# Six plain up-projection pairs instead of seven in the conv FFN of a two-layer encoder, the last three of them on the normalised stream

## The chip, the cores and the metric

The kernel runs on one core of one Trainium2 chip. The metric is device microseconds of one execution. TensorE (PE) does the matmuls, VectorE (DVE), ScalarE (ACT) and GpSimd (POOL) the rest, and SyncE (SP) issues the transfers. PEld is PE's loading of weights, which overlaps its matmuls.

## The reference, cut to what matters

Two layers; each has a mixer of two kinds of attention, a cross attention over 256 memory tokens, and a gated FFN with a convolution over positions. The change is in the FFN alone:

```python
def conv_ffn(h, w_up, conv_w, conv_b, w_down):
    u = h @ w_up
    up = jnp.pad(u, ((0, 0), (1, 1), (0, 0)))
    u = up[:, :-2] * conv_w[0] + up[:, 1:-1] * conv_w[1] + up[:, 2:] * conv_w[2] + conv_b
    gate, val = jnp.split(u, 2, axis=-1)
    return (jax.nn.silu(gate) * val) @ w_down
...
x = x + conv_ffn(rms_norm(x, norm_ffn[l]), w_up[l], conv_w[l], conv_b[l], w_down[l])
```

x is 512 positions by 1024 channels in float32; w_up is 1024 x 5632 and w_down 2816 x 1024.

## The kernel before

The stream x is kept transposed: eight tiles xT of 128 channels by 512 positions. Float32 accuracy comes from splitting each operand into hi (x rounded to the PE format fp32r) and lo = x - hi; each product is three matmuls, hi x hi, hi x lo and lo x hi (`mm3`, `product`). ACT writes hi, and DVE or POOL subtracts for lo.

Every call on an engine is first recorded, all at one source line (L404 in the profile). Then a planner sets one order of the whole program, from costs of its own, due times and the free buffers, and each engine runs its part of that order. So the code states what depends on what, and the planner decides where an instruction stands in its engine's queue. What limits it: three raw weight tiles (512 KB each, N_RAW), four hi and four lo weight tiles, 23 tiles called r, 14 tiles called t, two called xg, and eight PSUM banks (four mm, two sc, two tr).

The FFN of a layer computes 22 pairs: pair j is 128 gate channels and the 128 value channels that go with them. There are two ways to compute a pair.

- **Plain pairs** (j below N_PLAIN = 7, in `up_first`). Two gemms, one for each side: 8 channel tiles k, three matmuls each, with 512 columns. They read `ffn.ops`, hi/lo of the stream before its scaling by 1/rms, in the two xg tiles. So they can start before the norm is known; once it is known (`ffn.spread` makes rep in SBUF and a copy in PSUM), DVE multiplies both results by rep (`finish`).
- **Seven-product pairs** (`up`). A Strassen-like scheme on halves of the channels and of the positions: seven products of 4 x 3 matmuls with 256 columns. Its operands `right` come from the normalised stream (built in `operands`: a and b are channel tiles c and c + 4, scaled; hi/lo of parts of a and b, and of four sums t1 to t4). The weight side is built from two raw tiles in `combined`: three parts split into hi/lo in r tiles, and four sums, added by POOL and split in the hi and lo weight tiles by ACT and DVE.

After a pair, `up_finish` does the convolution on ACT and DVE, which reads the PSUM banks and so frees them, then silu(gate) x value; `store` writes hi/lo for the down projection. The stores of the plain pairs come after all plain pairs in the program, most of them into the two xg tiles (the ring), which are free once the last plain pair has read `ffn.ops`; j = 2 and 3 go into r tiles. Grouped down projections (`down_grouped`, 24 matmuls of 512 columns for each row r) are mixed in behind the seven-product pairs by `behind(n)`: row 0 after pair 7, one or two rows after each later pair.

SP issues the weight tiles in the order of the planner. A raw tile's slot is free when all splits and sums that read it are done.

Of the kernel before, what the change touches and what calls it, by code (L numbers as in the profile page):

```python
# [26 lines left out]
KC = D // P  # L27
# [3 lines left out]
D_FF = 2816  # L31
NF = D_FF // P
N_GROUPED = 16
N_PLAIN = 7
N_COLS = 256
BEHIND = 5
EPS = 1e-6
# [21 lines left out]
N_RAW, N_W, AHEAD, AHEAD_HELD, N_WARM, N_LATE, N_FIRST = 3, 4, 2, 5, 7, 4, (12, 22)  # L59


SLOTS = {j: j % KC if j < 8 or j > 11 else (2, 3, 0, 1)[j - 8] for j in range(N_GROUPED)}


def behind(n):

    at = lambda r: (7, 8, 9, 9, 10, 11, 12, 12)[r] if r < 8 else r + BEHIND
    return [r for r in range(N_GROUPED) if at(r) == n]


# [428 lines left out]
def encoder_kernel(ctx: ExitStack, tc: tile.TileContext, t: dict, out: list):  # L499
# [21 lines left out]
    def rtile(shape, dt=F32R):  # L521
        return rpool.tile([P, *shape], dt, tag="r", name=nm("r"), padded_shape=[P, *pad(shape)])
# [7 lines left out]
    def rpair():  # L530

        hl = rtile((2, S))
        return hl[:, 0, :], hl[:, 1, :]
# [13 lines left out]
    f = lambda ap: ap.bitcast(F32)  # L547
# [84 lines left out]
    at = 0  # L632
# [22 lines left out]
    def gemm_T(ps, w, ops, ks, first, last, c=slice(0, P)):  # L655
        wh, wl = w
        for k in ks:
            mm3(ps, wh[:, k, c], wl[:, k, c], *ops[k], k == first, k == last)
# [252 lines left out]
    for l in range(DEPTH):  # L911
# [602 lines left out]
        def up_project(j, side, ks, us):  # L1514
            if us[side] is None:
                us[side] = get_w(("up", j, side)), ps_mm() if j % 4 < 2 else ps_t() if side else ps_s()
            w, pm = us[side]
            gemm_T(pm, w, ffn.ops, ks, 0, KC - 1)

        def up_first():  # L1520


            us = [[None] * 2 for _ in range(N_PLAIN)]
            up_project(0, 0, range(KC - 1), us[0])
            ffn.stat()
            ffn.spread()
            up_project(0, 1, range(KC - 1), us[0])
            for side in range(2):
                up_project(0, side, [KC - 1], us[0])
            up_project(1, 0, range(KC), us[1])  # L1530
            built = operands()
            next(built)
            up_project(1, 1, range(KC), us[1])

            def finish(j):
                pms = [pm for _, pm in us[j]]
                for pm in pms:
                    DVE.tensor_mul(pm, pm, ffn.rep)
                return up_finish(j, pms)

            stores = []
            for j in range(2, N_PLAIN):
                for side in range(2):
                    up_project(j, side, range(KC), us[j])
                next(built, None)
                stores.append(finish(j - 2))
            for j in range(N_PLAIN - 2, N_PLAIN):
                stores.append(finish(j))
            for store in stores:
                store()  # L1550

        H = S // 2
        right = {n: [None] * 4 for n in ("11", "21", "22", "t1", "t2", "t3", "t4")}

        def operands():


            base = []
            for c in range(4):
                xs = []  # L1560
                for k in (c, c + 4):
                    v = tmp()
                    DVE.scalar_tensor_tensor(v, xT[k], par[:, l, G_FFN + k : G_FFN + k + 1], ffn.psum,
                                             op0=ALU.mult, op1=ALU.mult)
                    xs.append(v)
                a, b = xs
                i = c % 2
                if i == 0:
                    base = [rtile((4, H)) for _ in range(3)]
                pair = lambda t: t[:, 2 * i : 2 * i + 2].rearrange("p n q -> p (n q)")  # L1570
                ACT.copy(pair(base[0]), b)
                POOL.tensor_sub(pair(base[1]), b, f(pair(base[0])))
                ACT.copy(base[2][:, i], a[:, :H])
                DVE.tensor_sub(base[2][:, 2 + i], a[:, :H], f(base[2][:, i]))
                right["21"][c], right["22"][c] = ((base[0][:, 2 * i + n], base[1][:, 2 * i + n]) for n in range(2))
                right["11"][c] = base[2][:, i], base[2][:, 2 + i]
                one, two = tmp((2, H)), tmp((2, H))
                POOL.tensor_sub(one[:, 0], a[:, :H], a[:, H:])
                DVE.scalar_tensor_tensor(one[:, 1], one[:, 0], -1.0, b[:, H:], op0=ALU.mult, op1=ALU.subtract)
                POOL.tensor_sub(two[:, 0], b[:, H:], a[:, H:])  # L1580
                DVE.scalar_tensor_tensor(two[:, 1], one[:, 1], -1.0, b[:, :H], op0=ALU.mult, op1=ALU.subtract)
                hi, lo = rtile((4, H)), rtile((4, H))
                for n, v in ((0, one), (2, two)):
                    ACT.copy(hi[:, n : n + 2], v)
                    DVE.tensor_sub(lo[:, n : n + 2], v, f(hi[:, n : n + 2]))
                for n, name in enumerate(("t1", "t2", "t3", "t4")):
                    right[name][c] = hi[:, n], lo[:, n]
                yield
# [47 lines left out]
        def up_finish(j, us, turned=False):  # L1636
            cs = []
            for side in range(2):
                ch = side * NF + j
                u = us[side]  # L1640
                w = [par[:, l, CW + i * 2 * NF + ch : CW + i * 2 * NF + ch + 1] for i in range(3)]
                if turned and side:
                    w = [minus[:, l, i * NF + j : i * NF + j + 1] for i in range(3)]
                cc = tmp()
                ACT.activation(cc, u, AF.Identity, bias=par[:, l, CB + ch : CB + ch + 1], scale=w[1])
                for wi, dst, src in (
                    (w[0], slice(8, S), slice(0, S - 8)),
                    (w[0], slice(1, 8), slice(S - 8, S - 1)),
                    (w[2], slice(0, S - 8), slice(8, S)),
                    (w[2], slice(S - 8, S - 1), slice(1, 8)),  # L1650
                ):
                    DVE.scalar_tensor_tensor(cc[:, dst], u[:, src], wi, cc[:, dst], op0=ALU.mult, op1=ALU.add)
                cs.append(cc)
            ACT.activation(cs[0], cs[0], AF.Silu)
            DVE.tensor_mul(cs[0], cs[0], cs[1])

            def store():
                if j < N_GROUPED and j not in (2, 3):
                    if not ring:
                        ring.extend(xpool.tile([P, KC, S], F32R, tag="xg", name=nm("xg"), bufs=2) for _ in range(2))  # L1660
                    acts[j] = [v[:, SLOTS[j]] for v in ring]
                else:
                    acts[j] = rpair()
                hi, lo = acts[j]
                ACT.copy(hi, cs[0])
                DVE.tensor_sub(lo, cs[0], f(hi))

            return store
# [298 lines left out]
```

## Time and profile before

| what | us |
|---|---|
| median of 3 runs | 1303.92 |
| lowest and highest | 1303.55, 1304.28 |
| the profiled execution's own time | 1303.15 |
| its span, first to last instruction | 1301.1 |
| layer 0: the first gemm of the second plain pair starts | 312.37 |
| layer 0: the first seven-product pair starts | 377.90 |
| layer 1: the first seven-product pair starts | 1020.30 |

Times inside the execution are us from the start of the span. Groups are named out<-in by the program's tiles: sc<-xg is a matmul that writes an sc bank and reads an xg tile, t<-mm,par a part of the convolution, mm<-mm,rep the scaling of a plain pair's result. A row of the timeline gives the start, the length, engine, line, operation, tiles, shape and count; in brackets stand the engine's idle time before it and what ended it. Starts of matmuls that follow each other give the true time of one: their lengths overlap.

### The profile page before, as it was taken

The page shows a single profiled execution, that of the slowest core. Times are in us where ns is not written, and L with a number is a line of the kernel's source. Part 1 is how long each engine was busy: PE and PEld are TensorE (multiplying, and loading weights), DVE is VectorE, ACT ScalarE, POOL GpSimd, SP SyncE. Part 2 cuts the span into 40 slices and gives each one's busy share as a digit, 9 for nine tenths or more (in the row PEclk, how much of TensorE's full clock was granted, in tenths as well). Part 3 has the DMA queues.
Part 4 walks back from the last instruction along what each step waited for, and adds up shares of the span by engine and source line. Part 5 has one row for each costly group of instructions (what it writes and reads, how often), then busy time and mean ns, then how long its engine had stood idle before and what let it go on. Part 6 is the DMA issues. An engine that isn't in the chain of part 4 may idle for free.

```text
span 1301.1 us, 20672 instructions
## 1 busy us (share of the span) xinstructions
PE 1291.9 (99%) x7485; PEld 1135.6 (87%) x7485; DVE 1066.1 (82%) x1999; ACT 777.3 (60%) x1510; POOL 655.8 (50%) x523
## 2 busy tenths in 40 slices
PE   9999999999999999999999999999999999999998
PEld 8898888888889999999888988888888999999997
DVE  8679886768999998878655887866789998997784
ACT  7776686555565555555537867865655645554552
POOL 4565866716743334334626566765367224542260
PEclk9999999999999999999999999999999999999999
DMA  8651313313323333233356322232133233333231
GB/s 286 194 171 49 114 49 97 96 35 113 98 81 98 110 134 98 66 97 113 122 162 179 114 81 82 66 99 96 49 98 97 82 113 115 112 99 98 77 118 65
DMA packets 42901, 137.47 MB, mean 106 GB/s; under 512 B 5040, under 2 KB 8496, under 8 KB 42800
## 3 DMA queue, kind: packets, MB, share of 16 engines
q1 hardware_dynamic: 42224, 135.51, 33.3%
q8 instruction: 59, 0.97, 0.3%
q10 hardware_dynamic: 576, 0.66, 0.1%
q14 instruction: 42, 0.34, 0.1%
HBM read 126.18 MB, written 2.10 MB: 99 GB/s over the span
## 4 chain that ended last, share of the span: by engine, by line
PE 94%; POOL 1%; DVE 1%; issue 1%; ACT 1%; DMA 0%; SPq 0%; DVEq 0%; POOLq 0%
PE mm L404 55%; PE sc L404 20%; PE tr L404 20%; POOL lo L404 1%; ACT t L404 0%; POOL s L404 0%; DVE t L404 0%; DVE r L404 0%; DVE s L404 0%; DMA xT<-in_w 0%; ACT r L404 0%; POOL t L404 0%; DVE mm L404 0%; DVE sc L404 0%; POOL r L404 0%
## 5 line engine op out<-in xcount | busy, mean ns | idle before, releaser
L404 POOL TENSOR_TENSOR lo<-raw,hi 128x512 fp32r<-128x512 f32 (+2 forms) x168 | 265.8, 1599 | 185.8 <-ACT hi L404 179.9
L404 PE MATMUL mm<-xg,hi 128*128 128x512 f32 (+1 forms) x1026 | 319.3, 391 | 0.0
L404 POOL TENSOR_TENSOR t<-raw,raw 128x512 f32<-128x512 f32 x60 | 86.5, 1463 | 290.4 <-DMA raw<-in_w 213.8
L404 ACT CAST hi<-raw 128x512 fp32r<-128x512 f32 (+2 forms) x216 | 163.8, 784 | 111.8 <-PE mm L404 35.2
L404 PEld LDWEIGHTS mm<-xg,hi 128*128 128x128 f32 x1026 | 188.4, 188 | 35.5
L404 PE MATMUL mm<-xg,lo 128*128 128x512 f32 (+1 forms) x513 | 199.7, 389 | 0.0
L404 PE MATMUL mm<-r,hi 128*128 128x512 f32 (+1 forms) x608 | 192.0, 388 | 0.0
L404 PE MATMUL sc<-r,r 128*128 128x256 f32 (+1 forms) x736 | 131.8, 310 | 0.9 <-ACT t L404 0.9
L404 PEld LDWEIGHTS mm<-r,hi 128*128 128x128 f32 x608 | 111.9, 188 | 21.6 <-DVE xg L404 0.8
L404 PE MATMUL mm<-r,lo 128*128 128x512 f32 (+1 forms) x336 | 123.3, 367 | 0.0
L404 PEld LDWEIGHTS mm<-xg,lo 128*128 128x128 f32 x513 | 96.3, 188 | 20.2
L404 PEld LDWEIGHTS sc<-r,r 128*128 128x128 f32 x736 | 103.5, 191 | 7.4 <-ACT t L404 2.0
L404 PE MATMUL mm<-hi,xg 128*128 128x512 f32 (+1 forms) x384 | 108.1, 358 | 0.0
L404 PE MATMUL sc<-r,hi 128*128 128x256 f32 (+1 forms) x752 | 106.7, 288 | 0.0
L404 POOL TENSOR_SCALAR t<-t,s 128x512 f32<-128x512 f32 (+1 forms) x112 | 67.0, 613 | 71.8 <-DVE s L404 71.7
L404 POOL TENSOR_TENSOR t<-t,raw 128x512 f32<-128x512 f32 x60 | 99.5, 1658 | 4.7
L404 PEld LDWEIGHTS sc<-r,hi 128*128 128x128 f32 x752 | 97.0, 192 | 1.4
L404 PE MATMUL tr<-r,lo 128*128 128x256 f32 x720 | 96.2, 283 | 0.0
L404 PE MATMUL tr<-r,r 128*128 128x256 f32 x720 | 96.1, 283 | 0.0
L404 PEld LDWEIGHTS tr<-r,r 128*128 128x128 f32 x720 | 92.6, 191 | 2.3
L404 PEld LDWEIGHTS tr<-r,lo 128*128 128x128 f32 x720 | 90.7, 192 | 0.0
L404 ACT ACTIVATE t<-sc,s,s 128x512 f32<-128x512 f32 (+1 forms) x96 | 68.1, 711 | 29.2 <-DVE s L404 25.8
(158 smaller groups left out, 2756.3 us busy)
## 6 DMA issues: line engine op xcount, KB each, us to landing
raw<-in_w SPq DMA_DIRECT2D x207, 512.0 KB, 3.6
r<-r SPq DMA_DIRECT2D x30, 256.0 KB, 3.6
r<-in_bias SPq DMA_DIRECT2D x16, 384.0 KB, 4.6
raw<-in_w SPq DMA_DIRECT2D x8, 384.0 KB, 3.8
r<-in_memT SPq DMA_DIRECT2D x4, 512.0 KB, 7.2
xT<-in_w SPq DMA_DIRECT2D x7, 256.5 KB, 4.6
r<-in_w SPq DMA_DIRECT2D x9, 128.0 KB, 4.1
t<-in_memT SPq DMA_DIRECT2D x4, 256.0 KB, 6.1
```

What stands on the lines that cost most here:

```text
L404: call(*args, **kwargs)
```

## The change

Pair j = 6 becomes a seven-product pair. `operands` first builds the eight normalised tiles in full width, hi and lo (`normed`, eight r tiles), and the operands 11, 21 and 22 of the seven products become views of them; the sums t1 to t4 come afterwards, one c for each of the pairs j = 2 to 5. Plain pairs j = 3 to 5 read `normed` and need no multiplication by rep; j = 0 to 2 stay as they were. So the xg tiles are free after j = 2, and j = 3 alone is stored outside the ring. The grouped rows 0 to 7 stand one pair earlier, at pairs 6, 7, 8, 9, 9, 10, 11, 12.

```diff
-N_PLAIN = 7
+N_PLAIN = 6
+N_RAWS = 3
...
-SLOTS = {j: j % KC if j < 8 or j > 11 else (2, 3, 0, 1)[j - 8] for j in range(N_GROUPED)}
+SLOTS = {j: j % KC if j < 8 or j > 11 else (3, 0, 1, 2)[j - 8] for j in range(N_GROUPED) if j != 3}
...
-    at = lambda r: (7, 8, 9, 9, 10, 11, 12, 12)[r] if r < 8 else r + BEHIND
+    at = lambda r: r + BEHIND + (r < 4)
...
-            gemm_T(pm, w, ffn.ops, ks, 0, KC - 1)
+            gemm_T(pm, w, ffn.ops if j < N_RAWS else normed, ks, 0, KC - 1)
...
-                for pm in pms:
+                for pm in pms if j < N_RAWS else []:
                     DVE.tensor_mul(pm, pm, ffn.rep)
...
+        normed = [None] * KC
...
-            base = []
+            pairs = []
             for c in range(4):
                 xs = []
                 for k in (c, c + 4):
...
                     xs.append(v)
-                a, b = xs
-                i = c % 2
-                if i == 0:
-                    base = [rtile((4, H)) for _ in range(3)]
-                pair = lambda t: t[:, 2 * i : 2 * i + 2].rearrange("p n q -> p (n q)")
-                ACT.copy(pair(base[0]), b)
-                POOL.tensor_sub(pair(base[1]), b, f(pair(base[0])))
-                ACT.copy(base[2][:, i], a[:, :H])
-                DVE.tensor_sub(base[2][:, 2 + i], a[:, :H], f(base[2][:, i]))
-                right["21"][c], right["22"][c] = ((base[0][:, 2 * i + n], base[1][:, 2 * i + n]) for n in range(2))
-                right["11"][c] = base[2][:, i], base[2][:, 2 + i]
+                    hi, lo = normed[k] = rpair()
+                    ACT.copy(hi, v)
+                    (POOL if k == c else DVE).tensor_sub(lo, v, f(hi))
+                pairs.append(xs)
+                right["11"][c] = tuple(v[:, :H] for v in normed[c])
+                right["21"][c], right["22"][c] = (tuple(v[:, H * n : H * n + H] for v in normed[c + 4]) for n in range(2))
+            yield
+            for c, (a, b) in enumerate(pairs):
                 one, two = tmp((2, H)), tmp((2, H))
...
-                if j < N_GROUPED and j not in (2, 3):
+                if j in SLOTS:
```

What this does to the queues is shown at three places, all in layer 0. In the names the number tells one tile from another; the changed file is one line longer ahead of the helper, so its line reads L405.

PE, pair j = 6. Before, its gate side: a gemm of 24 matmuls with 512 columns that reads the xg tiles.

```order
L404 MATMUL sc_846<-xg_638,hi_835 128x512
L404 MATMUL sc_846<-xg_639,hi_835 128x512
L404 MATMUL sc_846<-xg_638,lo_836 128x512
L404 MATMUL sc_846<-xg_638,hi_835 128x512
L404 MATMUL sc_846<-xg_639,hi_835 128x512
```

Now, the first of its seven products: 12 matmuls with 256 columns that read halves of normalised tiles (r_772 to r_784) and a part of the weights (r_835), and the beginning of the second, on the sums.

```order
L405 MATMUL tr_866<-r_772,r_835 128x256 x3
L405 MATMUL tr_866<-r_776,r_835 128x256 x3
L405 MATMUL tr_866<-r_780,r_835 128x256 x3
L405 MATMUL tr_866<-r_784,r_835 128x256 x3
L405 MATMUL sc_865<-r_801,hi_842 128x256
L405 MATMUL sc_865<-r_802,hi_842 128x256
```

A gemm of wide matmuls has become a product of narrow ones.

DVE, right behind the spread of 1/rms (tr_761; rep_760 is its copy in SBUF). The rows t<-xT are the normalised stream, mm_753 to mm_790 the results of the first two pairs. Before:

```order
L404 TENSOR_TENSOR mm_753<-mm_753,rep_760 128x512
L404 TENSOR_TENSOR mm_766<-mm_766,rep_760 128x512
L404 SCALAR_TENSOR_TENSOR t_771<-xT_76,par,tr_761 128x512
L404 TENSOR_TENSOR mm_770<-mm_770,rep_760 128x512
L404 SCALAR_TENSOR_TENSOR t_772<-xT_78,par,tr_761 128x512
L404 TENSOR_TENSOR r_775<-t_771,r_775 128x256
L404 SCALAR_TENSOR_TENSOR t_792<-xT_76,par,tr_761 128x512
L404 SCALAR_TENSOR_TENSOR t_776<-t_776,t_772 128x256
L404 SCALAR_TENSOR_TENSOR t_798<-mm_753,par,t_798 128x504
L404 SCALAR_TENSOR_TENSOR t_777<-t_776,t_772 128x256
```

Now:

```order
L405 TENSOR_TENSOR mm_753<-mm_753,rep_760 128x512
L405 SCALAR_TENSOR_TENSOR t_773<-xT_78,par,tr_761 128x512
L405 TENSOR_TENSOR mm_766<-mm_766,rep_760 128x512
L405 SCALAR_TENSOR_TENSOR t_775<-xT_76,par,tr_761 128x512
L405 TENSOR_TENSOR r_774<-t_773,r_774 128x512
L405 SCALAR_TENSOR_TENSOR t_777<-xT_78,par,tr_761 128x512
L405 TENSOR_TENSOR mm_770<-mm_770,rep_760 128x512
L405 SCALAR_TENSOR_TENSOR t_779<-xT_77,par,tr_761 128x512
L405 TENSOR_TENSOR r_778<-t_777,r_778 128x512
L405 SCALAR_TENSOR_TENSOR t_781<-xT_79,par,tr_761 128x512
L405 SCALAR_TENSOR_TENSOR t_799<-t_799,t_773 128x256
```

All eight normalised tiles and their lo parts have moved ahead of the sums and of the first convolution.

DVE, ahead of the hi/lo operand from a weight sum (hi_885 before, hi_876 now) that the second seven-product pair reads in its second product. Before, where t_862 to t_865 are the convolutions of plain pairs j = 5 and 6:

```order
L404 TENSOR_TENSOR r_878<-raw_845,r_878 128x512
L404 SCALAR_TENSOR_TENSOR t_864<-sc_846,par,t_864 128x7
L404 SCALAR_TENSOR_TENSOR t_862<-mm_838,par,t_862 128x504
L404 SCALAR_TENSOR_TENSOR t_865<-tr_859,par,t_865 128x504
L404 SCALAR_TENSOR_TENSOR t_864<-sc_846,par,t_864 128x504
L404 SCALAR_TENSOR_TENSOR t_865<-tr_859,par,t_865 128x7
L404 TENSOR_TENSOR r_879<-raw_858,r_879 128x512
L404 SCALAR_TENSOR_TENSOR t_865<-tr_859,par,t_865 128x504
L404 TENSOR_TENSOR hi_885<-t_882,hi_885 128x512
```

Now, where r_860 is the store of j = 3, t_854 and t_855 belong to j = 4, t_856 and t_857 to j = 5, and tr_866 to the first seven-product pair:

```order
L405 TENSOR_TENSOR r_860<-t_852,r_860 128x512
L405 SCALAR_TENSOR_TENSOR t_855<-mm_826,par,t_855 128x7
L405 TENSOR_TENSOR r_869<-raw_833,r_869 128x512
L405 SCALAR_TENSOR_TENSOR t_856<-mm_834,par,t_856 128x504
L405 SCALAR_TENSOR_TENSOR t_857<-mm_847,par,t_857 128x504
L405 TENSOR_TENSOR tr_866<-tr_866,t_868 128x256
L405 TENSOR_TENSOR r_870<-raw_846,r_870 128x512
L405 SCALAR_TENSOR_TENSOR t_856<-mm_834,par,t_856 128x7
L405 SCALAR_TENSOR_TENSOR t_857<-mm_847,par,t_857 128x7
L405 TENSOR_TENSOR t_854<-t_854,t_855 128x512
L405 TENSOR_TENSOR hi_876<-t_873,hi_876 128x512
```

The operand now stands behind the work of pairs j = 3 to 5 and an addition of the first seven-product pair; before, behind the convolutions of j = 5 and 6.

## The prediction

> **What bounds the kernel now.** I read the page first (busy times, then the chain that ended last), then the table of busy time by stage, then the timelines of TensorE (PE) and VectorE (DVE) where the change lies.
>
> ```profile
> span 1301.1 us, 20672 instructions
> ...
> PE 1291.9 (99%) x7485; PEld 1135.6 (87%) x7485; DVE 1066.1 (82%) x1999; ACT 777.3 (60%) x1510; POOL 655.8 (50%) x523
> ...
> PE 94%; POOL 1%; DVE 1%; issue 1%; ACT 1%; DMA 0%; SPq 0%; DVEq 0%; POOLq 0%
> ```
>
> PE is busy 99% of the span and makes 94% of the chain: what other engines do costs nothing unless PE waits for it. The table by stage shows whether it does. Columns: the stretch, its length, then PE, PEld, DVE, ACT and POOL busy. Three rows are layer 0's FFN (plain pairs from 318.06 on; the first two seven-product pairs; most of the rest), three layer 1's.
>
> ```profile
> 318.06:377.90 59.84, 59.84 (x266) 49.55 (x265) 59.84 (x94) 34.53 (x52) 39.33 (x24) 1.00 0.27 87
> 377.90:407.53 29.63, 29.63 (x206) 27.70 (x204) 29.63 (x52) 19.44 (x35) 12.41 (x8) 1.00 0.27 84
> 407.53:555.00 147.47, 147.47 (x1007) 137.55 (x1006) 136.12 (x209) 79.28 (x139) 56.62 (x36) 1.00 0.33 104
> 959.00:1019.00 60.00, 60.00 (x267) 49.66 (x266) 59.34 (x93) 34.30 (x51) 39.21 (x24) 1.00 0.28 88
> 1019.00:1049.00 30.00, 30.00 (x207) 28.03 (x206) 30.00 (x52) 19.19 (x35) 12.20 (x8) 1.00 0.29 91
> 1049.00:1170.00 121.00, 121.00 (x813) 112.23 (x812) 114.17 (x175) 65.76 (x114) 52.60 (x32) 1.00 0.36 113
> ```
>
> PE has no idle time in the FFN (59.84 of 59.84, at granted clock 1.00), so there a matmul less is time less. But DVE is full too, for the first 90 us of each FFN (59.84 and 29.63 of the same stretches). It does not bound now; it has no reserve there either.
>
> **The change on TensorE.** A plain pair is two gemms of 8 x 3 matmuls of 512 columns, a seven-product pair 7 x 4 x 3 = 84 matmuls of 256. The seventh pair (j = 6) goes from the first kind to the second, once in each layer. PE's timeline gives the prices by the starts:
>
> ```profile
> 318.06 0.62 PE L404 MATMUL mm<-xg,hi 128*128 128x512 f32 x2
> ...
> 323.50 0.62 PE L404 MATMUL sc<-xg,hi 128*128 128x512 f32 x2
> ...
> 1154.06 1.59 PE L404 MATMUL tr<-r,r 128*128 128x256 f32 x12
> ...
> 1164.13 0.63 PE L404 MATMUL mm<-xg,hi 128*128 128x512 f32 x2
> ```
>
> A gemm of 24 lasts from 318.06 to 323.50: 5.44 us, 226.7 ns a matmul. The 84 last from 1154.06 to 1164.13: 10.07 us, 119.9 ns each. So a pair's exchange is worth 2 x 5.44 - 10.07 = 0.81 us, **1.6 us for both layers**. An eighth of the column work goes (24,576 to 21,504), but some 13 ns of each matmul do not shrink with its width, and 36 more of them give back 0.5 us.
>
> The Trainium skill ("TensorE: Matmul & The Clock Gate", Back-to-back issue gap) spaces warm matmuls by N/2.4 + 2.5 ns. An estimate by that page is 215.8 and 109.2 ns, so 1.19 us a layer and 2.4 us in all. Both rows above are 11 ns slower than the page, so this trace does not agree, and the sum keeps 1.6 us.
>
> The pairs j = 3 to 5 read normalised tiles instead of raw ones in the same 48 matmuls: nothing on PE.
>
> **The other engines.** Kinds are counted in the order of both kernels, and priced by DVE's groups from 317 to 405 us (mean ns of one after the comma). In a full queue a row takes some 0.07 us less than its mean, since neighbours overlap by that.
>
> ```profile
> L404 DVE SCALAR_TENSOR_TENSOR t<-mm,par,t 128x504 f32<-128x504 f32 x16 | 11.5, 728 | 0.0
> L404 DVE TENSOR_TENSOR r<-t,r 128x512 fp32r<-128x512 f32 x10 | 11.1, 1111 | 0.0
> L404 DVE TENSOR_TENSOR r<-raw,r 128x512 fp32r<-128x512 f32 x7 | 7.5, 1078 | 0.0
> L404 DVE TENSOR_TENSOR t<-t,t 128x512 f32<-128x512 f32 x7 | 7.1, 1028 | 0.0
> L404 DVE TENSOR_TENSOR mm<-mm,rep 128x512 f32<-128x512 f32 x8 | 5.3, 687 | 0.7 <-ACT rep L404 0.7
> L404 DVE TENSOR_TENSOR xg<-t,xg 128x512 fp32r<-128x512 f32 x5 | 4.9, 988 | 0.0
> L404 DVE TENSOR_TENSOR r<-t,r 128x256 fp32r<-128x256 f32 x4 | 3.5, 869 | 0.0
> L404 DVE TENSOR_TENSOR tr<-tr,t 128x256 f32<-128x256 f32 x1 | 0.4, 419 | 0.0
> ```
>
> Per layer DVE loses eight multiplications by rep (4.9 us in the queue) and four 256-wide lo subtractions (3.2). It gains three 512-wide subtractions in r from t (3.1), three from raw (3.0), four more in the weights' hi and lo tiles and an xg store (some 4), and two small adds (1). That is about +3 us in 237 us of FFN, where the first three stage rows have DVE busy for 225.6: no bound on average. ScalarE (ACT) gains eleven 512-wide casts and loses two 1024-wide, POOL gains four 512-wide sums and loses two 1024-wide subtractions; by the same rows ACT is busy 58% and POOL 66% of the plain stage, so PE's work hides both. SP issues as many transfers as before. I cost all this at nothing, as long as DVE's queue arrives in time.
>
> **Does it arrive?** This is the unknown. Seven-product pairs start one plain pair (10.88 us) earlier, and the eight normalised tiles are needed from the fourth pair on.
>
> The tiles come first. After the change the last of their subtractions on DVE is the 18th instruction of its queue (four rep products, seven normalised products, four subtractions, three shorter ones): by the groups 13.7 us. Counted from 317.49 (row below) that is 331.2, and the fourth pair starts three gemms of 5.44 us after 318.06, at 334.4. POOL has four subtractions and two weight tiles to do until then, some 11 us. No wait.
>
> The tight place is the second seven-product pair, whose second product needs a hi/lo operand made from a weight sum (hi<-t,hi):
>
> ```profile
> 317.49 1.30 DVE L404 TENSOR_TENSOR mm<-mm,rep 128x512 f32<-128x512 f32 x2 [0.66 <-ACT rep L404]
> ...
> 385.80 1.13 DVE L404 TENSOR_TENSOR hi<-t,hi 128x512 fp32r<-128x512 f32 x1
> 393.42 1.60 PE L404 MATMUL sc<-r,hi 128*128 128x256 f32 x12
> ```
>
> Now the operand is ready at 386.93 and PE takes it at 393.42: 6.5 us to spare. Up to it DVE's queue has 108 instructions, after the change 98. By kind: eight rep products less (4.9), four 256-wide (3.2), four of the conv and normalising kind (2.6); three r<-t more (3.1), and one each of t<-t, xg<-t and tr<-tr (2.2). The queue is 5.4 us shorter, PE comes 10.88 us earlier: **1.0 us is left**. In layer 1 the same stage rows stand, so I take the same. Below nothing the wait cannot go, since PE is full; above, it depends on how often DVE is held up by POOL:
>
> ```profile
> 358.15 2.40 POOL L404 TENSOR_TENSOR lo<-raw,hi 128x1024 fp32r<-128x1024 f32 x1 [1.98 <-ACT hi L404]
> 358.29 2.81 DVE L404 TENSOR_TENSOR r<-t,r 128x512 fp32r<-128x512 f32 x1
> ```
>
> The same subtraction that takes 1.11 us on the mean took 2.81 here: it began just behind a POOL subtraction and ended 0.6 us after it. Each such meeting more than before costs up to 2.81 - 1.11 = 1.7 us, of which 1.0 is covered once. I take no wait (the queue's sum is the nearest evidence, and up to this place POOL has two 1024-wide subtractions less) and keep 0 to 2.4 us a layer for the range.
>
> The Trainium skill ("SBUF — State Buffer", Who interferes with whom) says that a DVE instruction with two SBUF inputs and a GpSimd instruction that reads SBUF block each other for the whole instruction. The two rows agree (0.6 us behind POOL's end); by that rule the second rival below is a matter of which rows meet.
>
> **The sum.** The profiled execution took 1303.15 us (span 1301.1 and 2.05 around it). Less 1.6 is 1301.5. The median of the three timed runs, 1303.92, lies 0.77 above it, so against the median the forecast is 1302.3 us, 0.12% faster. A measurement here tells some 0.2% (2.6 us) from no change, so this counts as the same.
>
> **The rivals.** (1) The exchange holds and PE does not wait: 1302.3, own range 1301.5 to 1303.2. Chance 0.58.
>
> (2) DVE comes late to the first seven-product pairs and PE waits. It decides from 1.0 us of lateness; at 1.8 the gain is gone. One POOL meeting more in each layer (1.7) makes 0.7 of wait: 1302.3 + 1.4 = 1303.7, the same. Two make 3.4 - 1.0 = 2.4: 1302.3 + 4.8 = 1307.1, **slower**. For it speak DVE's full stretches and the 6.5 us that shrink to 1.0; against it that before the change PE waited nowhere there. Chance 0.13 for one, 0.11 for more.
>
> (3) The recorded order is planned anew as a whole, so other stages move too. PE's idle time stands outside the FFN (length, then PE busy):
>
> ```profile
> 0.00:20.00 20.00, 18.91 (x87) 15.85 (x88) 14.92 (x36) 16.25 (x35) 2.69 (x9) 1.00 0.87 275
> ...
> 120.00:140.00 20.00, 19.29 (x95) 15.33 (x95) 19.53 (x36) 11.37 (x21) 12.58 (x10) 1.00 0.19 58
> ...
> 260.00:280.00 20.00, 19.54 (x112) 16.37 (x111) 15.72 (x46) 13.66 (x34) 4.81 (x2) 1.00 0.19 58
> ...
> 900.00:920.00 20.00, 19.55 (x113) 16.49 (x112) 14.88 (x45) 13.16 (x34) 4.81 (x2) 1.00 0.26 82
> ```
>
> The three attention slices hold 0.71 + 0.46 + 0.45 = 1.6 us. If they all went: 1300.7, faster by 0.25%; if they doubled: 1303.9. Chance 0.11 and 0.05.
>
> (4) The narrow matmuls issue at the page's spacing after all: 1303.92 - 2.4 = 1301.5, the same. Against it stand 84 of them at 119.9 ns. Chance 0.02.
>
> **Numbers.** Faster by over 0.2% is the first half of (3) and a little of (1): 0.13. Slower is the second half of (2) and mishaps of its kind: 0.13. The same: 0.74. The range goes down to (3), 1300.5, and up into (2), 1306.0.
>
> **What would show it.** Right: 84 more narrow and 48 fewer wide matmuls a layer, PE full from the fourth pair to the last, the FFN 0.8 us shorter. Wrong: idle time of PE ahead of a product of the first three seven-product pairs, ended by DVE (hi, lo or r) or by POOL's t, or ahead of the fourth pair, ended by an r tile; then (2) holds. A difference outside the FFN is (3).

## The result and the profile after

| | before | after |
|---|---|---|
| median of 22 runs each, us | 1303.56 | 1301.36 |
| lowest and highest | 1302.95, 1304.63 | 1300.42, 1303.79 |
| the profiled execution | 1303.15 | 1302.85 |

The ratio of the times is 0.9984, with a 95% interval from 0.9977 to 0.9991: 2.1 us faster (1.2 to 3.0), within 2% and so counted as the same. After's runs spread over 3.4 us, before's over 1.7, and its profiled execution is one of its longer ones.

The page of the kernel after, its span, busy times and the chain:

```profile
span 1300.8 us, 20807 instructions
...
PE 1290.8 (99%) x7557; PEld 1138.5 (88%) x7557; DVE 1076.1 (83%) x2001; ACT 784.4 (60%) x1526; POOL 659.5 (51%) x527
...
PE 91%; DVE 5%; issue 2%; POOL 2%; ACT 1%; DVEq 0%; POOLq 0%; ACTq 0%
```

PE has 72 matmuls more (2 x 84 - 2 x 48), as planned. New is the chain's 5% on DVE: somewhere DVE sets the pace. The table by stage of the kernel after shows where (the columns are those of the table before):

```profile
20.00:40.00 20.00, 18.77 (x85) 15.30 (x84) 16.35 (x29) 12.60 (x22) 11.17 (x10) 1.00 0.70 248
120.00:140.00 20.00, 19.64 (x99) 16.16 (x98) 18.34 (x36) 11.47 (x22) 15.17 (x11) 1.00 0.18 58
260.00:280.00 20.00, 20.00 (x113) 16.63 (x112) 15.80 (x46) 13.57 (x34) 4.80 (x2) 1.00 0.18 60
318.00:378.00 60.00, 60.00 (x300) 51.13 (x300) 60.00 (x92) 37.51 (x58) 38.45 (x25) 1.00 0.26 82
378.00:408.00 30.00, 30.00 (x213) 28.28 (x212) 30.00 (x52) 16.82 (x31) 11.43 (x8) 1.00 0.35 106
...
640.00:660.00 20.00, 19.64 (x87) 15.67 (x86) 11.99 (x20) 8.15 (x14) 13.43 (x12) 1.00 0.42 134
900.00:920.00 20.00, 20.00 (x116) 16.89 (x116) 15.59 (x46) 14.16 (x36) 4.80 (x2) 1.00 0.24 79
959.00:1019.00 60.00, 60.00 (x300) 51.17 (x299) 58.82 (x90) 37.58 (x58) 36.12 (x23) 1.00 0.26 82
1019.00:1049.00 30.00, 29.15 (x204) 27.16 (x204) 30.00 (x49) 16.48 (x30) 11.43 (x9) 1.00 0.32 102
```

Layer 0's FFN is full, as it was. Four things stand out against before. Layer 1's FFN has a hole (a stretch in which PE stands idle) of 0.85 us in 1019:1049. Three attention slices that the change doesn't touch have lost idle time: 0.36, 0 and 0 us, where before had 0.71, 0.46 and 0.45. The start of layer 1 (640:660) has gained 0.36 us of idle time, and the program's start (20:40) 1.23 us; both slices were full before.

The first plain gemm and the next layer's first gemm give layer 0's FFN from start to start ("FFN 0" below). Layer 1's FFN ends with the program, so it is counted from its first gemm to the start of the program's last group of matmuls ("FFN 1"). PE's timeline, before and then after:

```profile
301.24 0.61 PE L404 MATMUL mm<-xg,hi 128*128 128x512 f32 x2
...
649.08 0.62 PE L404 MATMUL sc<-xg,hi 128*128 128x512 f32 x2
...
943.65 0.62 PE L404 MATMUL mm<-xg,hi 128*128 128x512 f32 x2
...
1290.85 4.35 PE L404 MATMUL mm<-r,r 128*128 128x512 f32 x18
```

```profile
301.01 0.62 PE L405 MATMUL mm<-xg,hi 128*128 128x512 f32 x2
...
648.09 0.62 PE L405 MATMUL sc<-xg,hi 128*128 128x512 f32 x2
...
942.81 0.62 PE L405 MATMUL mm<-xg,hi 128*128 128x512 f32 x2
...
1290.49 4.38 PE L405 MATMUL mm<-r,r 128*128 128x512 f32 x18
```

In layer 0, 347.84 us became 347.08: the exchange is worth 0.76 us where nothing waits. In layer 1, 347.20 us became 347.67: the FFN with the hole is 0.5 us longer than before. The hole, on PE's timeline after:

```profile
1022.67 1.60 PE L405 MATMUL tr<-r,r 128*128 128x256 f32 x12
1024.11 0.40 PE L405 MATMUL sc<-r,hi 128*128 128x256 f32 x2
1025.35 1.46 PE L405 MATMUL sc<-r,hi 128*128 128x256 f32 x10 [0.85 <-DVE hi L405]
```

This is the place that the prediction called tight: the second product of the second seven-product pair. Two of its matmuls have run with the hi half of the weight sum; the third needs the lo half, which DVE writes late. Why it is late stands 30 us earlier. The timeline of all engines after:

```profile
990.26 3.00 POOL L405 TENSOR_TENSOR lo<-raw,hi 128x1024 fp32r<-128x1024 f32 x1 [3.56 <-ACT hi L405]
...
993.22 3.00 POOL L405 TENSOR_TENSOR t<-raw,raw 128x512 f32<-128x512 f32 x2
...
994.99 0.62 ACT L405 CAST hi<-t 128x512 fp32r<-128x512 f32 x1 [3.25 <-POOL t L405]
...
995.65 1.11 DVE L405 TENSOR_TENSOR hi<-t,hi 128x512 fp32r<-128x512 f32 x1 [1.06 <-ACT hi L405]
```

The brackets are read from the bottom up: DVE stood still for 1.06 us because ACT's cast was late, ACT for 3.25 because POOL's weight sum was late, and POOL for 3.56 because of an earlier cast of ACT. DVE's queue has no pause afterwards and never makes up for the 1.06 us, and PE meets them at 1024. In layer 0 DVE ended at the same place 0.4 us ahead of the product, and 0.6 us ahead of its third matmul (timeline of all engines after):

```profile
381.26 0.68 DVE L405 TENSOR_TENSOR hi<-t,hi 128x512 fp32r<-128x512 f32 x1
...
382.32 0.88 PE L405 MATMUL sc<-r,hi 128*128 128x256 f32 x6
```

### The profile page after: what moved, and what is told of

It is laid out like the page before. It is cut to its first block, busy times and chain, and to the rows that moved or that the text cites. A ratio compares the mean times of both kernels' runs of the same rounds, so it can differ in the third digit from the quotient of the medians.

```text
span 1300.8 us, 20807 instructions
## 1 busy us (share of the span) xinstructions
PE 1290.8 (99%) x7557; PEld 1138.5 (88%) x7557; DVE 1076.1 (83%) x2001; ACT 784.4 (60%) x1526; POOL 659.5 (51%) x527
## 4 chain that ended last, share of the span: by engine, by line
PE 91%; DVE 5%; issue 2%; POOL 2%; ACT 1%; DVEq 0%; POOLq 0%; ACTq 0%
PE mm L405 52%; PE tr L405 20%; PE sc L405 19%; DVE t L405 2%; DVE r L405 1%; POOL lo L405 1%; DVE lo L405 0%; DVE s L405 0%; POOL s L405 0%; POOL t L405 0%; ACT r L405 0%; ACT t L405 0%; DVE mm L405 0%; DVE xg L405 0%; DVE hi L405 0%
## 5 line engine op out<-in xcount | busy, mean ns | idle before, releaser
L405 POOL TENSOR_TENSOR lo<-raw,hi 128x512 fp32r<-128x512 f32 (+2 forms) x164 | 255.9, 1579 | 161.6 <-ACT hi L405 153.9
L405 PE MATMUL mm<-xg,hi 128*128 128x512 f32 (+1 forms) x930 | 289.7, 392 | 0.0
L405 POOL TENSOR_TENSOR t<-raw,raw 128x512 f32<-128x512 f32 x64 | 99.1, 1569 | 284.2 <-DMA raw<-in_w 231.1
L405 ACT CAST hi<-raw 128x512 fp32r<-128x512 f32 (+2 forms) x212 | 159.6, 779 | 109.2 <-issue 37.2
L405 PE MATMUL mm<-r,hi 128*128 128x512 f32 (+1 forms) x704 | 222.0, 388 | 0.0
L405 PEld LDWEIGHTS mm<-xg,hi 128*128 128x128 f32 x930 | 170.8, 189 | 31.9
L405 PE MATMUL mm<-xg,lo 128*128 128x512 f32 (+1 forms) x465 | 181.3, 390 | 0.0
L405 PEld LDWEIGHTS mm<-r,hi 128*128 128x128 f32 x704 | 130.2, 188 | 25.9 <-DVE xg L405 0.8
L405 PE MATMUL mm<-r,lo 128*128 128x512 f32 (+1 forms) x384 | 141.5, 369 | 0.0
L405 PE MATMUL sc<-r,r 128*128 128x256 f32 (+1 forms) x760 | 133.9, 309 | 0.0
L405 PE MATMUL sc<-r,hi 128*128 128x256 f32 (+1 forms) x832 | 122.9, 291 | 0.8 <-DVE hi L405 0.8
L405 PEld LDWEIGHTS sc<-r,hi 128*128 128x128 f32 x832 | 109.0, 192 | 3.6 <-DVE hi L405 1.0
L405 PEld LDWEIGHTS sc<-r,r 128*128 128x128 f32 x760 | 106.0, 191 | 6.3 <-ACT t L405 0.6
L405 PE MATMUL tr<-r,lo 128*128 128x256 f32 (+1 forms) x784 | 108.9, 285 | 0.0
L405 PE MATMUL mm<-hi,xg 128*128 128x512 f32 (+1 forms) x384 | 108.1, 357 | 0.0
L405 POOL TENSOR_TENSOR t<-t,raw 128x512 f32<-128x512 f32 x64 | 102.7, 1605 | 5.0
L405 PEld LDWEIGHTS mm<-xg,lo 128*128 128x128 f32 x465 | 87.5, 188 | 18.2
L405 POOL TENSOR_SCALAR t<-t,s 128x512 f32<-128x512 f32 (+1 forms) x112 | 66.9, 611 | 71.7 <-DVE s L405 68.4
L405 PE MATMUL tr<-r,r 128*128 128x256 f32 x768 | 102.7, 283 | 0.0
L405 PEld LDWEIGHTS tr<-r,r 128*128 128x128 f32 x768 | 98.9, 191 | 2.6
L405 PEld LDWEIGHTS tr<-r,lo 128*128 128x128 f32 x784 | 99.7, 192 | 0.8
L405 DVE TENSOR_TENSOR r<-raw,r 128x512 fp32r<-128x512 f32 x96 | 91.3, 956 | 0.2 <-ACT r L405 0.2
```

The source lines that it names most:

```text
L405: call(*args, **kwargs)
```

## The experiments

What moved the attention slices? The planner tries 24 orders: two patiences, each with three margins (in ns; the lateness it allows for every instruction), each in four rounds. It keeps the one with the lowest mean of its own trial runs. For the kernel before that was patience 60, margin 160, round 3; for the change it was patience 60, margin 120, round 2. I call these the old and the new setting. The theories: A, DVE's queue is late at the tight place; B, that wait comes and goes between runs; C, a wait that is removed there turns up elsewhere; D, the planner's setting moved the other stages; E, the normalised tiles did.

All results in one table, times in us. FFN 0 and FFN 1 are the times of the two FFNs as counted above, from the profile of each kernel; "attention" is PE's idle time in 120:140, 260:280 and 900:920 (the last one ten us later for p3 and e4, whose layer 1 starts some seven us later).

| kernel | plain pairs; setting (patience, margin, round) | median | ratio to before, 95% interval | FFN 0 | FFN 1 | attention |
|---|---|---|---|---|---|---|
| before | 7; 60, 160, 3 | 1303.56 | | 347.84 | 347.20 | 1.62 |
| after | 6; 60, 120, 2 | 1301.36 | 0.9984, 0.9977 to 0.9991 | 347.08 | 347.67 | 0.36 |
| again | 6; 60, 120, 2 | 1301.49 (one run) | | 347.08 | 347.75 | 0.36 |
| e1 | 6, old operands; 60, 160, 4 | 1303.40 | 1.0001, 0.9993 to 1.0010 | 347.86 | 347.23 | 1.61 |
| e2 | 7, normalised; 120, 120, 2 | 1302.44 | 0.9993, 0.9984 to 1.0001 | 347.85 | 347.92 | 0.35 |
| p2 | 7, normalised; 60, 160, 3 | 1303.25 | 0.9999, 0.9990 to 1.0008 | 347.84 | 347.40 | 1.62 |
| p5 | 7, normalised; 60, 120, 2 | 1302.61 | 0.9992, 0.9983 to 1.0001 | 347.99 | 347.69 | 0.36 |
| p1 | 6; 60, 160, 3 | 1303.92 | 1.0001, 0.9992 to 1.0010 | 348.13 | 347.44 | 1.60 |
| p3 | before; 60, 120, 2 | 1315.56 | 1.0084, 1.0071 to 1.0096 | 355.71 | 352.50 | 0.36 |
| e3 | 6, s1 late; 120, 120, 2 | 1303.69 | 1.0001, 0.9992 to 1.0011 | 348.65 | 347.14 | 0.35 |
| p4 | 6, s1 late; 60, 160, 4 | 1304.57 | 1.0009, 1.0000 to 1.0018 | 348.60 | 347.74 | 1.62 |
| p6 | 6, s1 late; 60, 120, 2 | 1301.31 | 0.9982, 0.9973 to 0.9991 | 347.31 | 346.36 | 0.36 |
| d1 | 6, four raw; 60, 120, 2 | 1303.79 | 0.9999, 0.9990 to 1.0007 | 349.80 | 346.86 | 0.36 |
| e4 | 5; 60, 120, 2 | 1316.35 | 1.0097, 1.0081 to 1.0112 | 356.02 | 354.13 | 0.36 |

### The changed kernel once more

> The changed kernel once more, for a second profile. Theory A (VectorE's queue arrives late at the second seven-product pair of layer 1 as a rule): TensorE again idles 0.7 to 1.3 us there, span 1300 to 1301.5 us. Rival B (that wait comes and goes from run to run, and this is what spreads the runs from 1300.4 to 1303.8 us): if the span is below 1299.5 us, the wait there is under 0.3 us.

It came out at 1301.49 us, span 1299.7, near the median; the span lies just below what A had. Two stages of its table:

```profile
20.00:40.00 20.00, 20.00 (x91) 16.47 (x90) 17.31 (x31) 13.28 (x23) 11.25 (x9) 1.00 0.72 242
...
1019.00:1049.00 30.00, 29.16 (x206) 27.25 (x205) 30.00 (x50) 16.18 (x29) 11.24 (x8) 1.00 0.33 103
```

The hole in layer 1 is there again with 0.84 us. What is gone is the first profile's 1.23 us of idle time in 20:40, and the difference of the two spans (1.1 us) has nearly its size. So at least part of the spread belongs to the program's start. The expectation asked for a span below 1299.5 to judge B, and this one wasn't; whether the shortest runs lack the hole stays open.

### Six pairs by six or seven, old or new setting

e1 is the kernel before with six pairs, and with the change's slots and `behind` (which leaves rows 3 and 7 at pairs 9 and 12 and moves the other six of the first eight rows one pair ahead):

```diff
-N_PLAIN = 7
+N_PLAIN = 6
-SLOTS = {j: j % KC if j < 8 or j > 11 else (2, 3, 0, 1)[j - 8] for j in range(N_GROUPED)}
+SLOTS = {j: j % KC if j < 8 or j > 11 else (3, 0, 1, 2)[j - 8] for j in range(N_GROUPED) if j != 3}
...
-    at = lambda r: (7, 8, 9, 9, 10, 11, 12, 12)[r] if r < 8 else r + BEHIND
+    at = lambda r: r + BEHIND + (r < 4)
...
-                if j < N_GROUPED and j not in (2, 3):
+                if j in SLOTS:
```

> Six plain pairs, but with the operands of before: all six read the raw stream and are multiplied by rep, and the seven-product operands are tiles of their own. If only TensorE's exchange counts (0.81 us a layer): 1303.6 - 1.6 = 1302.0 us. If VectorE's queue is the limit at the second seven-product pair: it has six rep products more (3.7 us) than the changed kernel and 256-wide instead of 512-wide subtractions (0.9 less), so 2.8 us more in each layer; the changed kernel had 0.4 us left in layer 0 and 1.0 us of wait in layer 1, so TensorE waits 2.4 and 3.8 us there and the time is 1301.4 + 5.2 = 1306.6 us. If neither counts and the gain came from the other stages' new order, no forecast from these terms.

e2 is the changed kernel with N_PLAIN = 7 and before's SLOTS and `behind`.

> Seven plain pairs as before, but pairs 4 to 7 read the normalised tiles. If the gain is TensorE's exchange: no gain, 1303.6 us (1303.2 to 1304.0), TensorE without idle time in the feed-forward stretches. If the gain came from the normalised tiles (fewer rep products on VectorE, earlier free tiles) or from the other stages: 1301.4 to 1302.5 us.

e1 missed both of its numbers. It gained nothing, but lost much less than 5.2 us: its FFN 0 takes 347.86 us, so the exchange was given back whole. Its stage rows show 0.28 us of PE's idle time in each layer's first seven-product pairs, ended by DVE; the rest of the 0.8 us doesn't show as idle time. e2 fell into its second range, which doesn't tell the tiles from the other stages: 0.9 us less without the exchange (its interval just includes no gain). Its FFN 0 is as before, but its attention slices are those of the changed kernel. The planner had picked margin 160 for e1 and 120 for e2, which speaks for theory D, so the next batch held the setting. p1 is the changed kernel, p2 is e2, both with

```diff
-PLANS = [((60.0, *[patience] * 3, 0.0), 300, margin, ASIDE, 4) for patience in (60.0, 120.0) for margin in (80.0, 120.0, 160.0)]
+PLANS = [((60.0, *[60.0] * 3, 0.0), 300, 160.0, ASIDE, 3)]
```

and p3 is the kernel before, with 120.0 in place of 160.0, two rounds, and the second kept. p5 is e2 with that setting.

> The changed kernel, its order planned with the one setting that the planner had picked for the kernel before (margin 160, third round) instead of the one that it picked for the change (margin 120, second round). Theory D (the planner's other pick moved the idle time outside the feed-forward network, and the spread of the runs): TensorE's idle time is as before in the slices 120:140, 260:280 and 900:920 (0.7, 0.46, 0.45 us by the stage rows) and near nothing at 640:660, and the runs spread no wider than 1.7 us; the exchange gives 1.6 us, less what VectorE's lateness costs under this order (0 to 1.3 us): 1301.8 to 1303.1 us. Rival E (the normalised tiles themselves thinned out the other stages): those slices stay at the changed kernel's lower values and the time is 1300.5 to 1301.4 us.

> Seven plain pairs, pairs 4 to 7 on normalised tiles, planned with the setting of the kernel before. Theory D: 1303.4 us (1303.0 to 1303.8), since 1302.4 came from the planner's pick and not from the tiles. Rival E: 1302.4 us again. With the first kernel of this batch the difference is the exchange alone: 1.6 us if VectorE is in time.

> The kernel before, nothing changed but the planner's setting: margin 120, second round, as picked for the change. Theory D: TensorE's idle time in the attention slices and at the start of layer 1 is that of the changed kernel, and the runs spread by over 2.5 us. Its feed-forward stages may wait more than before, so no total is forecast. Rival E: attention slices as before.

> Seven plain pairs, pairs 4 to 7 on normalised tiles, planned with the setting picked for the change (margin 120, second round). This fills the table of six or seven pairs by old or new setting. Theory D: the other stages' gain comes with the setting alone; against the changed kernel the exchange is missing (+1.6 us) and so is the wait in layer 1 (-1.3 us): 1301.7 us, TensorE idle nowhere in the feed-forward stages. Rival (the gain needs six pairs): 1303.3 us as with the old setting.

The attention slices settle it. p2's stages (seven pairs, old setting):

```profile
120.00:140.00 20.00, 19.28 (x96) 15.37 (x95) 19.54 (x37) 10.98 (x22) 12.10 (x10) 1.00 0.22 63
260.00:280.00 20.00, 19.55 (x112) 16.44 (x111) 15.63 (x44) 13.66 (x34) 4.81 (x2) 1.00 0.20 66
...
640.00:660.00 20.00, 20.00 (x91) 16.58 (x90) 12.32 (x21) 8.35 (x15) 14.99 (x13) 1.00 0.48 155
900.00:920.00 20.00, 19.55 (x111) 16.44 (x111) 14.87 (x44) 12.85 (x34) 4.99 (x3) 1.00 0.29 91
```

and p3's (the kernel before, new setting; its layer 1 starts some seven us later, so the windows there are ten us later):

```profile
120.00:140.00 20.00, 19.64 (x98) 16.15 (x97) 18.32 (x36) 11.75 (x22) 15.71 (x12) 1.00 0.23 62
260.00:280.00 20.00, 20.00 (x114) 16.62 (x113) 15.27 (x42) 13.61 (x36) 4.81 (x2) 1.00 0.17 54
...
660.00:680.00 20.00, 19.64 (x88) 15.69 (x87) 13.48 (x25) 7.50 (x14) 4.00 (x5) 1.00 0.55 172
910.00:930.00 20.00, 20.00 (x113) 16.60 (x112) 15.86 (x46) 13.49 (x33) 4.82 (x2) 1.00 0.19 60
```

The idle time follows the setting: 1.60 to 1.62 us in all five rows with margin 160, 0.35 to 0.36 in all nine with 120, with six or seven pairs, normalised tiles or not. For these slices D is shown and E has fallen. The 0.36 us at the start of layer 1 are there in p3 and p5 too, but not in p6, which has the same setting (640:660 full): they come with single orders. Where they are there, the setting is worth 1.26 - 0.36 = 0.9 us outside the FFN by these four slices. Inside it takes some back: p5's FFNs are 0.15 and 0.29 us longer than p2's. And the kernel before couldn't use it: p3's FFNs hold 5.5 and 3.3 us of PE's idle time, and it is 0.8% slower. With the normalised tiles the FFN of seven pairs bears it (p5).

The four corners, by medians: seven pairs 1303.25 (old) and 1302.61 (new), six pairs 1303.92 (old) and 1301.36 (new). The exchange gained 1.25 us with the new setting and lost 0.67 with the old one. By the intervals of the ratios (some 1.1 us to each side) neither is clear of noise; what stands behind them is read from the traces. p2 came in as D had it. p5's 1302.61 missed the expected 1301.7 by 0.9, about the size of that interval, and p1's 1303.92 lies above D's range of 1301.8 to 1303.1. p1's traces say why the old setting gains nothing:

```profile
360.00:380.00 20.00, 19.19 (x119) 17.21 (x118) 20.00 (x37) 11.15 (x20) 4.62 (x3) 1.00 0.26 80
...
1000.00:1020.00 20.00, 19.24 (x120) 17.24 (x119) 20.00 (x37) 13.26 (x23) 4.21 (x4) 1.00 0.25 78
```

There is a hole of 0.8 us in each layer, this time in the first seven-product pair. PE waits there not for DVE, but for ACT (timeline of all engines, p1):

```profile
371.43 0.21 DVE L405 SCALAR_TENSOR_TENSOR t<-sc,par,t 128x7 f32<-128x7 f32 x1
...
371.74 0.63 ACT L405 ACTIVATE t<-t 128x512 f32<-128x512 f32 x1 [2.33 <-DVE t L405]
...
372.27 0.35 ACT L405 COPY t<-sc 128x256 f32<-128x256 f32 x1
...
372.68 0.51 PE L405 MATMUL sc<-r,r 128*128 128x256 f32 x2 [0.81 <-ACT t L405]
```

ACT's silu of an earlier pair waits 2.33 us for DVE's convolution (the row at 371.43 ends at 371.64). Behind it in ACT's queue stands the copy out of bank sc that the next product on PE needs. That is DVE's lateness too, by way of ACT, though ACT is only 60% busy.

### Taking the late operand away

In e3, p4 and p6 the product that reads the raw part 12 is second, and s1 comes fourth:

```diff
-            product(v, w["s1"], "t1", True)
-            ACT.copy(p5, v)
+            product(y, w["12"], "21", True)
             finish_up()
+            product(v, w["s1"], "t1", False)
+            ACT.copy(p5, v)
             product(x, w["s2"], "t2", False)
             ACT.copy(sums[:, 1], x)
-            product(y, w["12"], "21", False)
```

> The changed kernel with the product that needs only a raw weight tile put second and the one with the weight sum s1 fourth, so VectorE has 24 matmuls of 119.9 ns, 2.9 us, more for the operand that was late. Theory A: no idle time of TensorE at the second seven-product pair in either layer; 1.0 us less where the wait was, so 1300.4 us, and a narrower spread. Rival B (the wait is in part of the runs): 1300.6 to 1301.0 us with no run above 1302. Rival C (the wait only moves to the next late operand): 1301.4 us, idle time at the next product.

> The changed kernel with the product of the sum s1 put fourth, planned with the setting margin 160. Theory A: no idle time at the second seven-product pair, none at 457 us (that belonged to the other setting); the full exchange of 1.6 us and other stages as before: 1301.8 us with a spread under 1.7 us. Rival C (a late operand later in the queue takes its place): 1302.5 to 1303.4 us with idle time at another product of the first four pairs.

> The changed kernel with the product of the sum s1 put fourth, planned with the changed kernel's own setting (margin 120, second round). Theory A: the 1.0 to 1.3 us of idle time in 1020:1040 go and nothing else changes: 1300.1 to 1300.4 us. Rival C (a later operand of VectorE's queue takes its place, as with the two other settings): 1301.2 to 1302.5 us, idle time at another product of the first four seven-product pairs.

The stage of p6 with the tight place of layer 1:

```profile
1020.00:1040.00 20.00, 20.00 (x140) 18.73 (x139) 20.00 (x34) 12.00 (x22) 7.87 (x5) 1.00 0.32 102
```

There is no hole, its FFN 1 is 1.3 us shorter than the changed kernel's, and its profiled execution is the shortest of all (span 1298.5). But p6 doesn't show which of two things removed the hole: the edit gives the operand more time, and in the order planned anew DVE's pause of 1.06 us is gone as well. And its median, 1301.31, is that of the changed kernel, where 1300.1 to 1300.4 was expected. So the price of the hole in a median run is not shown. (The median lies in rival C's range, but C's sign, idle time at another product, isn't in the trace.)

With the two other settings the wait turned up at another product, as rival C says, though both times lie above C's: e3 waits 1.06 us at 458.35 and p4 0.6 us in each layer, both for ACT's t as in p1. p4 is 0.65 us above p1 (its order is of the fourth round, p1's of the third); for e3 there is no kernel without the edit at its setting. Its runs spread from 1301.1 to 1306.7.

### More work in DVE's queue, and five pairs

d1 sets N_RAWS = 4, e4 sets N_PLAIN = 5 (with one more call of the generator of `operands`); both at the new setting.

> The changed kernel at its own setting with the fourth pair on the raw stream as well: two more multiplications by rep in VectorE's queue of each layer, 0.61 us each, 1.2 us. Theory A (VectorE's queue decides at the second seven-product pair): layer 0 had 0.4 us left and now waits 0.8 us, layer 1 waits 2.2 instead of 1.0 us: 1301.4 + 2.0 = 1303.4 us. Rival (the wait in layer 1 is a matter of single collisions with GpSimd and not of the queue's length): 1301.0 to 1302.0 us.

> One pair more is exchanged: five plain pairs, the setting of the changed kernel. TensorE's sum alone: 1.6 us less, 1299.8 us. Theory A: up to the second seven-product pair VectorE loses one plain pair's work (4.6 to 5.0 us) while TensorE arrives 10.88 us earlier, so 5.9 to 6.3 us more lateness in each layer: waits of 5.5 to 5.9 us in layer 0 and 6.9 to 7.3 us in layer 1, 1309 to 1313 us.

Timelines of POOL, DVE and PE of d1:

```profile
379.74 2.99 POOL L404 TENSOR_TENSOR t<-t,raw 128x512 f32<-128x512 f32 x2
...
381.51 1.77 DVE L404 TENSOR_TENSOR hi<-t,hi 128x512 fp32r<-128x512 f32 x1
...
382.16 0.40 PE L404 MATMUL sc<-r,hi 128*128 128x256 f32 x2
383.33 1.46 PE L404 MATMUL sc<-r,hi 128*128 128x256 f32 x10 [0.77 <-DVE hi L404]
...
454.82 1.69 PE L404 MATMUL tr<-r,lo 128*128 128x256 f32 x12 [1.00 <-ACT t L404]
```

Layer 0 waits 0.77 us at the tight place, where 0.8 was expected, but not in the expected way. The order was planned anew, and up to the operand DVE's queue has 98 instructions as in the changed kernel: two more multiplications by rep, but one t<-t and one t<-mm,par row less. These 98 take 66.88 us, 1.95 more than the changed kernel's, where 1.2 was expected. Over half of that is the operand's own row: 1.77 us beside two weight sums of POOL, where the changed kernel's took 0.68 (381.26 above). In layer 1 the same 98 take 63.65 us and PE does not wait at this place: 1000:1040 is full, where 2.2 us of wait were expected. So in layer 0 a collision with POOL is seen, as the rival has it, and that the queue's length decides is not shown. The 1303.79 us hit the expected 1303.4 by luck, and partly through another wait, the 1.00 us at 454.82.

e4 is slower than even A had it. Two stages of its table:

```profile
360.00:380.00 20.00, 16.70 (x111) 15.68 (x112) 18.08 (x34) 10.47 (x20) 5.38 (x4) 0.91 0.13 41
...
1000.00:1020.00 20.00, 16.55 (x114) 15.06 (x113) 18.87 (x38) 13.86 (x25) 8.93 (x6) 1.00 0.07 27
```

Its FFN 0 is 8.9 us longer than the changed kernel's. PE's recorded waits, 6.9 us in layer 0 and 7.2 in layer 1, come near A's, but stand at five places in each layer, ended by DVE or by ACT's t, and a stretch at a lower clock (0.91 in 360:380) comes on top. So at this setting DVE can't bear the exchange of one more pair; e4's order under other settings was not run.

## Why the prediction was right, and where it was not

The forecast was 1302.3 us, a change too small to tell; the median is 1301.36, 0.16% below before. So it came near, but its reasons held only in part, and two misses nearly cancel: the wait in layer 1 and the idle time that went elsewhere. That is luck. By the prediction's own signs its first rival did not hold: PE waited for DVE's hi in layer 1, which is rival (2), and the slices outside the FFN moved, which is (3).

- **The PE term held.** 0.76 us in layer 0 against 0.81. In layer 1 the wait hides it: FFN 1 takes 347.67 us, as with seven pairs at the same setting (p5, 347.69). In p6, without the hole, it takes 346.36: 0.84 less than before, 1.33 less than p5.
- **"No wait" failed in layer 1.** The step was: 98 instructions by their mean durations, 1.0 us left, the same for layer 1. It failed twice. First, the means: from its first multiplication by rep up to the operand the queue became 4.5 us shorter in layer 0 (69.43 to 64.93), not 5.4. PE came 10.6 us earlier, counted from the same start, and 0.4 us were left. The five r<-raw rows in it, as many as before, took 7.4 us instead of 4.8. Second, it treated DVE's queue as always full. The 98 instructions lay without a pause in layer 0, but held two in layer 1, of 1.06 and 0.13 us, and took 66.49 us there; PE waited 0.85. The prediction named POOL's meetings with DVE as the only thing that could hold DVE up; the pause of 1.06 us was a hand-over from POOL to ACT to DVE.
- **The price of a meeting was too low.** The mean of 1.11 us already holds meetings; an undisturbed subtraction of this size took 0.68 (381.26 above). So the one of 2.81 us lost 2.1 us, not 1.7.
- **"PE's work hides both" (ACT and POOL) was too quick.** It went by busy shares of 58% and 66%. In an order without spare time the place in the queue counts: POOL stood idle for 3.56 us ahead of the late sum, and in p1 ACT's copy stood behind a silu that waited for DVE.
- **The tiles were in time, but not as worked out.** There is no idle time ahead of the fourth pair. But in the profile after the 18th instruction of DVE's queue ended at 333.76 in layer 0, not at 331.2 (two of its subtractions, at 319.51 and 331.52, took 2.52 and 2.24 us instead of 1.11), and the fourth pair started at 334.15: it had 0.4 us to spare instead of 3.2.
- **Rival (3) came true, next to the forecast.** The attention slices lost 1.26 us of their 1.62 us and the start of layer 1 gained 0.36. The chance of 0.11 stood for all of it going. What decides it was not in the change's arithmetic: the planner picked another setting.

Together, by the profile before and the second profile of the changed kernel, from marker to marker:

| stretch | before | after | difference |
|---|---|---|---|
| start to layer 0's FFN | 301.24 | 299.77 | -1.47 |
| FFN 0 | 347.84 | 347.08 | -0.76 |
| layer 0's end of FFN to layer 1's FFN | 294.57 | 294.79 | +0.22 |
| FFN 1 | 347.20 | 347.75 | +0.55 |
| the last matmuls | 10.29 | 10.32 | +0.03 |
| span | 1301.14 | 1299.70 | -1.44 |

The named terms make -0.76 and about -0.8 (exchange), -1.26 and +0.37 (setting), +0.84 (wait), in all -1.6. That is near -1.44, but not stretch by stretch: ahead of layer 0's FFN the slices explain 0.81 of 1.47 us, and in FFN 1 exchange and wait make nothing, where 0.55 was measured. p5, with seven pairs at the same setting, has 0.49 there too (0.22 of it as idle time), but p6, also at that setting, has -0.84; so this goes with single orders, and its cause is open. The medians differ by 2.2 us (interval 1.2 to 3.0). What makes the shortest runs of the changed kernel 0.9 us shorter in span than this profile (1298.8 against 1299.7) isn't settled. Part of the distance to the forecast is its starting point: it took 1303.92, the median of three runs, where 22 runs have 1303.56.

## What to carry to other kernels

Where a planner orders the whole program, a local change is two changes: compare stages that it does not touch, and run it once with the planner's choice held, before crediting the change with the difference. A slack worked out from a full queue holds only while nothing in that queue waits; follow each input of the tight instruction back through the engines that make it, however low their busy share. An expectation that comes out by its number is not yet right in its way: count the queue again in the new order (d1). An exchange that only PE's sum justifies has to stop where the engine that feeds PE has nothing to spare.

## What the runs showed of the hardware

A stall of PE can cost more than its length. In p3 PE's timeline shows 24 matmuls behind a wait of 3.23 us that are slower than elsewhere:

```profile
391.12 2.44 PE L403 MATMUL sc<-r,r 128*128 128x256 f32 x12 [3.23 <-ACT t L403]
393.36 2.39 PE L403 MATMUL sc<-r,hi 128*128 128x256 f32 x12
395.59 0.63 PE L403 MATMUL mm<-r,hi 128*128 128x512 f32 x2
```

They took 4.47 us from start to start, where 24 at 119.9 ns take 2.88: 1.6 us on top of the wait. The stages of two us show the granted clock there:

```profile
392.00:394.00 2.00, 2.00 (x11) 2.00 (x10) 2.00 (x7) 1.42 (x4) 0.00 (x0) 0.50 0.00 0
394.00:396.00 2.00, 2.00 (x12) 1.96 (x12) 2.00 (x5) 1.07 (x3) 0.00 (x0) 0.71 0.00 0
```

The Trainium skill ("TensorE: Matmul & The Clock Gate", Part 1: The HAM clock gate) says that the clock falls to half after an idle window of about 3.4 us, and that this window runs freely. The half clock agrees; here 3.23 us were enough, and 3.27 us in layer 1 (0.57 and 0.58 in 1040:1042 and 1042:1044). In e4 two waits of 1.57 and 2.05 us, five us apart, did it too (0.91 in 360:380), while its waits in 1000:1020, of 1.41 and 2.04 us, left the clock at 1.00. The holes of the changed kernel, of 0.85 and 1.23 us, left it at 1.00.

The spread between runs seems to go with the planner's margin as well: 0.9 to 1.8 us over the five kernels with 160, 2.4 to 5.5 over the seven with 120 that had five runs or more (e4, with four runs, 0.8). The line is not sharp: the 27 runs of the kernel before that were taken beside p5, p6, d1 and e4 spread by 2.4 us. One cause is seen, the wait of 1.23 us in 20:40 that one profile of the changed kernel has and the other has not; the rest is open.
